# Ten full-array fp32 products of the identity, read by nothing, in TensorE's opening

## The chip, the cores and the metric

The kernel runs on one core of a Trainium2 chip. A core has five engines that run side by side and wait for one another by semaphores: TensorE (PE in the profile; its weight loads are shown apart as PEld), VectorE (DVE), ScalarE (ACT), GpSimd (POOL) and SyncE (SP), which here only issues transfers. The metric is the time of one execution on the device in microseconds (us), as the median of several runs.

## The reference, cut to what matters

One layer of a hybrid encoder is applied to two inputs with shared weights: a prompt of 512 tokens and a sample of 1024 tokens, 1024 channels each, all in fp32.

```python
def encoder_layer(x, norm_g, w_in, qn_a, kn_a, rpb_a, qn_b, kn_b, sink_b, w_o_a, w_o_b, w_out, t5_table):
    h = rmsnorm(x, norm_g)
    proj = h @ w_in
    qa, ka, va, za, qb, kb, vb, zb, ga, gb = jnp.split(proj, np.cumsum(SPLITS)[:-1], axis=-1)
    ...
    oa = neighbourhood_attention(qa, ka, va, rpb_a) * jax.nn.silu(za)
    oa = oa @ w_o_a
    ...
    ob = window_gqa_attention(qb, kb, vb, t5_table, sink_b) * jax.nn.silu(zb)
    ob = ob @ w_o_b
    merged = jax.nn.sigmoid(ga) * oa + jax.nn.sigmoid(gb) * ob
    return x + merged @ w_out
```

Before anything else can be multiplied, h must exist: each token's 1024 channels are scaled by one over the root of their mean square and by the gain norm_g.

## The kernel before, in words

Every large product is made of three TensorE products: each fp32 operand is split into a high part and a rest (whi and wlo for weights, hh and hl for h), and the kernel adds whi·hh, wlo·hh and whi·hl. ScalarE makes the high parts by a copy into the reduced type, VectorE or GpSimd subtracts to get the rests.

The prompt comes first (norm, projections, two attentions, dense part), then the sample. In the opening, which is all that the change touches, the work is this:

- Two constants are made: the identity `ident` (128 by 128, GpSimd, by a helper in masks.py) and a row of ones (VectorE, L417). The row of norm gains is fetched to one partition (L1621) and spread over 128 partitions by four fp32 products with the row of ones (L1629, contraction over one row, 256 columns each; the trace holds two records for each fp32 product).
- The prompt is normed in four tiles t of 128 tokens (`norm_tile`). For each: ScalarE squares and sums the tile (L460), GpSimd makes the scale (L464, L468), VectorE multiplies by scale and gain (L520), TensorE transposes blocks of 128 by 128 with `ident` (L532), ScalarE copies the result to hh (L537), VectorE makes hl (L542). Tile t=0 goes in four pairs of blocks, k0 = 0, 2, 4, 6; the other tiles in two halves of four blocks.
- The projection of tile t (L761, stationary operand from h, 384 columns of weights moving) takes eight blocks k with three products each. Its weights come in pieces of two blocks; ScalarE makes whi (L602), VectorE or GpSimd wlo (L607).
- ScalarE also copies the spread gain from PSUM to SBUF for the later tiles (L1641).

What sets the order: the class `Flow` collects all operations with a priority, an assumed cost and their dependencies, plays the program through once with these costs while it is being built, and issues each operation on its engine in the order in which it started there. The order on each engine is thus fixed when the kernel is built; on the chip each engine takes its own list strictly in turn, and semaphores hold an instruction until its inputs are there. A `bank("d")` is the one PSUM bank of the kind d; banks x and p are of other kinds.

In the kernel before, a function `wake` stands ready to issue pairs of transposes into a d bank, but its count WAKE is 0, so it issues nothing.

Of the kernel before, what the change touches and what calls it, by code (L numbers as in the profile page):

```python
# [29 lines left out]
SIDE = {5: 0, 8: 1, 11: 2, 15: 3}  # L30
CLASSIC_S = (1, 0, 2)
LEFT_PAD = 56
WAKE = 0
SOON = 10
RAW = {512: 2, 1024: 1}
WAKE_PRIO = 2
START = (-10, -6.5, -4, -3)
GATE = 2
FIRST_POOL = (0,)
# [1 line left out]
P = 128  # L41
# [313 lines left out]
def encoder_kernel(  # L355
# [26 lines left out]
    pe = nc.tensor  # L382
# [7 lines left out]
    ident = cpool.tile([P, P], F32, tag="ident", name="ident")  # L390
# [38 lines left out]
    f = Flow(pspool)  # L429

    def bank(tag):
        return f.value(pspool, [P, 512], F32, tag, BANKS[tag])
# [3 lines left out]
    gx_v = Value(None, None, None, "gx", 1)  # L436
    line_op, expanded = [], {}

    def wake():

        ps = bank("d")
        for i in range(WAKE):
            f.op(
                (("pe", 427),),
                lambda e, i=i: [pe.transpose(ps.t[:, j * P : (j + 1) * P], ident, ident) for j in range(2)],
                WAKE_PRIO, **({"into": [ps]} if i else {"new": [ps]}),
            )

    def rstd(pool, x, t, prio, load_prio, bufs, after=(), load_after=(), out=None):

        val = lambda shape, dt, tag, n: f.value(pool, shape, dt, tag, n)
        xt = val([P, D], F32, "xt", bufs)
        junk = val([P, D], mybir.dt.bfloat16, "junk", 1)
        ss, v = (val([P, 1], F32, "n" + n, bufs) for n in "sv")
        r = out or val([P, 1], F32, "nr", bufs)
        rv = lambda: r.t[:, t : t + 1] if out else r.t
        f.dma(lambda: nc.sync.dma_start(xt.t, x[t * P : (t + 1) * P, :]), 524288, load_prio, new=[xt], after=load_after)
        f.op(
            (("act", ACT_(D) + 93),),
            lambda e: act.activation(junk.t, xt.t, AF.Square, accum_out=ss.t), prio, new=[junk, ss], use=[xt], after=after,  # L460
        )
        f.op(
            (("pool", 164),),
            lambda e: nc.gpsimd.tensor_scalar(v.t, ss.t, 1.0 / D, EPS, op0=ALU.mult, op1=ALU.add),  # L464
            prio, new=[v], use=[ss],
        )
        f.op(
            (("pool", 464),), lambda e: nc.gpsimd.tensor_tensor(rv(), v.t, mhalf[:, :1], op=ALU.pow),  # L468
            prio, use=[v], **({"into": [r]} if out and t else {"new": [r]}),
        )  # L470
        return xt, r
# [33 lines left out]
    def norm_tile(pool, x, gb, gains_row, hh, hl, t, prio, load_prio, after=(), load_after=()):  # L505

        xt, r = rstd(pool, x, t, prio, load_prio, 4, after, load_after)
        tok = slice(t * P, (t + 1) * P)
        step, out = 2 if t == 0 else 4, []
        for k0 in range(0, KC, step):  # L510
            n, cols, ks = step * P, slice(k0 * P, (k0 + step) * P), slice(k0, k0 + step)
            ps, made = gains_row[k0 // 4]
            if t == 0:
                c = slice(k0 % 4 * P, k0 % 4 * P + n)
                gv, kw = lambda ps=ps, c=c: ps.t[:, c], {"use": [r], "hold": [xt, ps], "after": [made[k0 % 4 // 2]]}
            else:
                gv, kw = lambda cols=cols: gb.t[:, cols], {"use": [r], "hold": [xt, gb], "after": made, "port": True}
            m = f.op(
                (("dve", DVE_(n) + 60),),
                lambda e, cols=cols, gv=gv: dve.scalar_tensor_tensor(  # L520
                    xt.t[:, cols], xt.t[:, cols], r.t, gv(), op0=ALU.mult, op1=ALU.mult
                ),
                prio, **kw,
            )
            if t == 0:
                made.append(m)
            ps = bank("x")

            def emit(e, k0=k0, ps=ps):
                for i in range(step):  # L530
                    k = k0 + i
                    pe.transpose(ps.t[:, i * P : (i + 1) * P], xt.t[:, k * P : (k + 1) * P], ident)  # L532

            f.op((("pe", 109 * step),), emit, prio, new=[ps], after=[m], hold=[xt])
            pv = lambda ps=ps, n=n: ps.t[:, :n].rearrange("p (k n) -> p k n", n=P)
            a = f.op(
                (("act", ACT_(n, False)),), lambda e, ks=ks, pv=pv: act.activation(hh.t[:, ks, tok], pv(), AF.Copy),  # L537
                prio, use=[ps], hold=[hh],
            )
            b = f.op(  # L540
                (("dve", DVE_(n)),),
                lambda e, ks=ks, pv=pv: dve.tensor_tensor(  # L542
                    hl.t[:, ks, tok], pv(), hh.t[:, ks, tok].bitcast(F32), op=ALU.subtract
                ),
                prio, use=[ps], after=[a], hold=[hh, hl],
            )
            out += [a, b]
        return out
# [1067 lines left out]

    f.stage(-1000, open=(r_h, d0["p"], rb_pool, early["p"], late["p"], norm_p), make=h_p)
    f.dma(lambda: nc.sync.dma_start(gx, norm_g), 4096, 1, into=[gx_v])
    wake()
    gb = f.value(rb_pool, [P, NT_S], F32, "rb", 1)  # L1620
    row = f.dma(lambda: nc.sync.dma_start(gb.t[:1], norm_row.unsqueeze(0)), 4096, START[0] + 0.1, new=[gb])  # L1621
    gains_row = []
    for i in range(2):
        ps, made = bank("x"), []
        for j in range(2):
# [3 lines left out]
                lambda e, ps=ps, cols=cols, out=out: pe.matmul(ps.t[:, out], one, gb.t[:1, cols], start=True, stop=True),  # L1629
# [3 lines left out]
    for t in range(gp.nb):  # L1633
        h_ops["p"][t] = norm_tile(
            norm_p, x_p, gb, gains_row, *h_p, t, NORM[t], START[t], h_ops["p"][t - GATE][::2] if t >= GATE else (),
            h_ops["p"][0][-1:] if t > 1 else (),
        )
        for i, (ps, users) in enumerate(gains_row if t == 0 else ()):
            gains_row[i][1] = [f.op(
                (("act", ACT_(512, False)),),  # L1640
                lambda e, ps=ps, i=i: act.activation(gb.t[:, i * 512 : i * 512 + 512], ps.t, AF.Copy),  # L1641
                NORM[1] - 1, use=[ps], hold=[gb], after=users[2:],
            )]
    setup(norm_p, -0.7, h_ops["p"][1][:1])
    expand_ops(gp, [max(-1, (h // 2 - 1) * gp.nb) for h in range(8)], [h_ops["p"][t][:1] for t in (1, 3, 3, 3)])
    o_p, exps, start = attention_phase(gp, *h_p, h_ops["p"], mask_p, early["p"], late["p"])
    rb = f.value(rb_pool, [P, NT_S], F32, "rb", 1)
    r_s = f.value(norm_p, [P, gs.nb], F32, "r_s", 1)
    for t in range(gs.nb):
        at = 6 + 2 * t  # L1650
        rstd(norm_p, x_s, t, at, at, 4, (), [f.begun[NT_P, at - 2]], r_s)
    ps, r_t = bank("x"), f.value(norm_p, [gs.nb, P], F32, "r_t", 1)
# [4 lines left out]
    o = f.dma(lambda: nc.sync.dma_start(r_d, r_t.t), 4096, 20, use=[r_t])  # L1657
    f.dma(
        lambda: nc.sync.dma_start(rb.t, r_d.rearrange("t p -> (t p)").partition_broadcast(P)), 524288, 24, new=[rb],
        after=[o, f.begun[NT_P, 23]],  # L1660
# [21 lines left out]
    o_s, exps, start = attention_phase(gs, *h_s, h_ops["s"], mask_s, early["s"], late["s"])  # L1682
# [89 lines left out]
```

## Time and profile before

| | |
|---|---|
| median of 3 runs | 1145.79 us (1144.96 to 1147.68) |
| profiled execution, from the first to the last instruction (span) | 1144.7 us |
| what the runs' median has beyond this span | 1.1 us |
| TensorE busy in the span | 1133.8 us (99%) |
| VectorE, ScalarE, GpSimd busy | 854.4, 644.9, 308.3 us |
| TensorE busy in the first 30 us | 24.61 us |
| first product of the projection starts | 10.92 us |

Times in the trace are counted from the span's start. The profiled execution's own time is known by its span alone; it is compared with the runs through the 1.1 us in the table. In a timeline the first number is the start, the second how long the instruction or a merged group of them (xN) took. [...]

### The profile page before, as it was taken

What the parts mean: (1) busy time and instruction counts of PE and PEld (TensorE: products, weight loads), DVE (VectorE), ACT (ScalarE), POOL (GpSimd) and SP (SyncE); (2) the same over time, 40 slices, a digit from 0 to 9 for tenths busy, and PEclk for the clock granted to TensorE, in tenths of its full rate; (3) what the DMA queues carried; (4) which work ended last, traced back from release to release, by engine and by line L of the source; (5) the groups of instructions that cost most, each with busy time, mean ns of one, the idle gap of its engine ahead of it and who ended that gap; (6) DMA issues with size and microseconds to landing.
All of it is one profiled execution on the core that took longest, in us unless ns stands there. A gap on an engine that the chain in (4) does not pass through costs nothing.

```text
span 1144.7 us, 18482 instructions
## 1 busy us (share of the span) xinstructions
PE 1133.8 (99%) x6139; PEld 985.8 (86%) x6139; DVE 854.4 (75%) x1975; ACT 644.9 (56%) x1467; POOL 308.3 (27%) x413
## 2 busy tenths in 40 slices
PE   8999999999999999999999999999999999999998
PEld 6999988888888899999999888888888888788887
DVE  5888798497765468887778888865878755497984
ACT  5777987544433346665678988865534434343320
POOL 3653433000010054343333445330222210132110
PEclk9999999999999999999999999999999999999999
DMA  7854543488786422121221213226657335573072
GB/s 253 273 158 141 181 113 102 115 264 266 232 277 199 165 72 67 25 70 32 71 61 50 56 37 93 56 66 214 218 148 211 129 111 159 200 238 121 29 223 90
DMA packets 124705, 159.86 MB, mean 140 GB/s; under 512 B 28297, under 2 KB 66961, under 8 KB 124610
## 3 DMA queue, kind: packets, MB, share of 16 engines
q1 hardware_dynamic: 124610, 158.69, 45.4%
q8 instruction: 48, 0.79, 0.3%
q14 instruction: 47, 0.39, 0.1%
HBM read 121.93 MB, written 41.44 MB: 143 GB/s over the span
## 4 chain that ended last, share of the span: by engine, by line
PE 94%; DVE 2%; DMA 2%; ACT 1%; POOL 1%; issue 0%; SPq 0%; ACTq 0%; POOLq 0%
PE p L761 25%; PE x L1285 9%; PE x L1286 9%; PE x L1284 9%; PE x L1063 5%; PE x L1026 5%; PE x L934 4%; PE p L1284 4%; PE p L1285 4%; PE d L1284 4%; PE p L1286 4%; PE d L1286 4%; PE d L1285 4%; PE x L861 2%; DMA ot<-u_d 1%; DMA w<-in_w_att_dram 1%
## 5 line engine op out<-in xcount | busy, mean ns | idle before, releaser
L761 PE MATMUL p<-whi,hh 128*128 128x384 f32 x384 | 133.4, 348 | 0.0
L761 PE MATMUL p<-wlo,hh 128*128 128x384 f32 x384 | 133.1, 347 | 0.0
L761 PE MATMUL p<-whi,hl 128*128 128x384 f32 x384 | 132.4, 345 | 0.0
L978 ACT ACTIVATE sb<-sb,mx 128x384 f32<-128x384 f32 (+1 forms) x192 | 107.5, 563 | 22.4 <-DVE mx L969 22.2
L1167 ACT ACTIVATE whi<-raw 128x512 fp32r<-128x512 f32 (+1 forms) x140 | 81.1, 590 | 52.6 <-PE x L1285 26.2
L761 PE MATMUL p<-whi,hb 128*128 128x384 f32 x384 | 107.5, 347 | 0.0
L1172 POOL TENSOR_TENSOR wlo<-raw,whi 128x512 fp32r<-128x512 f32 (+1 forms) x29 | 40.9, 1413 | 242.4 <-ACT whi L1167 130.4
L1284 PE MATMUL x<-hh,whi 128*128 128x512 f32 x264 | 102.7, 389 | 0.0
L1285 PE MATMUL x<-hl,whi 128*128 128x512 f32 x264 | 102.7, 389 | 0.0
L1286 PE MATMUL x<-hh,wlo 128*128 128x512 f32 x264 | 102.7, 389 | 0.0
L1037 DVE TENSOR_TENSOR pp<-x,pp 128x512 fp32r<-128x512 f32 (+1 forms) x136 | 82.6, 638 | 18.9 <-ACT pp L1032 17.8
L1172 DVE TENSOR_TENSOR wlo<-raw,whi 128x512 fp32r<-128x512 f32 (+1 forms) x111 | 70.1, 645 | 30.5 <-ACT whi L1167 30.2
L1285 PE MATMUL x<-T,whi 128*128 128x512 f32 x224 | 87.5, 390 | 0.3 <-DVE T L1172 0.2
L1286 PE MATMUL x<-T,wlo 128*128 128x512 f32 x224 | 87.2, 389 | 0.0
L1284 PE MATMUL x<-T,whi 128*128 128x512 f32 x224 | 87.1, 389 | 0.0
L1032 ACT ACTIVATE pp<-x 128x512 fp32r<-128x512 f32 (+1 forms) x136 | 70.9, 560 | 22.8 <-PE x L1026 21.8
L799 POOL TENSOR_TENSOR rs_r<-rs_v,mhalf 128x4 f32<-128x4 f32 (+1 forms) x72 | 81.7, 1134 | 5.7
L1063 PE MATMUL x<-pp,v 128*128 128x256 f32 (+1 forms) x368 | 77.8, 324 | 0.8 <-DVE pp L1037 0.8
L792 POOL TENSOR_SCALAR rs_v<-ss 128x4 f32<-128x4 f32 (+1 forms) x72 | 26.2, 364 | 187.3 <-DVE ss L785 184.6
L761 PEld LDWEIGHTS p<-whi,hl 128*128 128x128 f32 x384 | 73.0, 190 | 1.3 <-issue 1.0
L761 PEld LDWEIGHTS p<-wlo,hh 128*128 128x128 f32 x384 | 73.0, 190 | 1.0 <-issue 0.5
L761 PEld LDWEIGHTS p<-whi,hh 128*128 128x128 f32 x384 | 73.0, 190 | 0.9 <-issue 0.5
(351 smaller groups left out, 2985.5 us busy)
## 6 DMA issues: line engine op xcount, KB each, us to landing
raw<-in_w_g_dram SPq DMA_DIRECT2D x76, 256.0 KB
w<-in_w_att_dram SPq DMA_DIRECT2D x46, 384.0 KB
ot<-o_d SPq DMA_DIRECT2D x36, 256.0 KB
g_d<-C SPq DMA_DIRECT2D x34, 256.0 KB
raw<-in_w_z_dram SPq DMA_DIRECT2D x32, 256.0 KB
raw<-in_w_out_dram SPq DMA_DIRECT2D x32, 256.0 KB
C<-g_d SPq DMA_DIRECT2D x24, 256.0 KB
out_dram<-C SPq DMA_DIRECT2D x23, 256.0 KB
```

What stands on the lines that cost most here:

```text
L761: pe.matmul(ps.t[:, :GW], part[u](k), mv.t[:, c], start=k == 0 and m == 0, stop=k == KC - 1 and m == 2,)
L799: lambda e: nc.gpsimd.tensor_tensor(r.t[:, :nn], rv.t[:, :nn], mhalf[:, :nn], op=ALU.pow),
L978: act.activation(sb.t[:, :width], sb.t[:, :width], AF.Exp, bias=mx.t[:, i : i + 1], scale=-1.0, accum_out=sm.t[:, i : i + 1],)
L1026: pe.transpose(pt.t[:, u * P : (u + 1) * P], sbs[i].t[:, c * P : (c + 1) * P], ident)
L1032: lambda e, pt=pt, pp=pp, nn=nn: act.activation(pp.t[:, 0, :nn], pt.t[:, :nn], AF.Copy),
L1037: lambda e, pt=pt, pp=pp, nn=nn: dve.tensor_tensor(pp.t[:, 1, :nn], pt.t[:, :nn], pp.t[:, 0, :nn].bitcast(F32), op=ALU.subtract),
L1063: pe.matmul(out(), v.t[:, vs], mv(), start=first, stop=last)
L1167: (("act", ACT_(n)),), lambda e: act.activation(hi(), src(), AF.Copy), prio,
L1172: lambda e: engines[e].tensor_tensor(lo(), src(), hi().bitcast(F32), op=ALU.subtract), prio,
L1284: pe.matmul(out, hi.t[:, cs], mh(), start=first and k == 0, stop=False)
L1285: pe.matmul(out, hi.t[:, cs], ml(), start=False, stop=False)
L1286: pe.matmul(out, lo.t[:, cs], mh(), start=False, stop=last and k == len(ws) - 1)
```

## The change

`wake` now issues plain fp32 products instead of transposes: the identity as the stationary and as the moving operand, 128 rows by 128 columns, into one d bank that no one reads. It is called twice. Seven products are put at the front of the whole program by their priority; three follow the second pair of transposes of tile t=0. The scheduler is told that they cost nothing, so that everything else is placed as before.

```diff
-WAKE = 0
+WAKE = (7, 3)
...
-WAKE_PRIO = 2
...
-    def wake():
-
-        ps = bank("d")
-        for i in range(WAKE):
+    idle = bank("d")
+
+    def wake(n, prio, after=()):
+
+        for _ in range(n):
             f.op(
-                (("pe", 427),),
-                lambda e, i=i: [pe.transpose(ps.t[:, j * P : (j + 1) * P], ident, ident) for j in range(2)],
-                WAKE_PRIO, **({"into": [ps]} if i else {"new": [ps]}),
+                (("pe", 0),), lambda e: pe.matmul(idle.t[:, :P], ident, ident, start=True, stop=True), prio, after=after,
+                **({"into": [idle]} if idle.writers else {"new": [idle]}),
             )
...
-            f.op((("pe", 109 * step),), emit, prio, new=[ps], after=[m], hold=[xt])
+            o = f.op((("pe", 109 * step),), emit, prio, new=[ps], after=[m], hold=[xt])
+            if t == 0 and k0 == 2:
+                wake(WAKE[1], -1000, [o])
...
-    wake()
+    wake(WAKE[0], -1000)
```

The order on TensorE at the start of the program, before: x is a PSUM bank, rb and one the gain row and the row of ones, xt the normed tile, p the projection's bank.

```order
L1762 UNCONDITIONAL_BRANCH [waits barrier_Pool_Activation_PE_DVE_SP_release]
L1629 MATMUL x<-rb,one 128x256 [waits DMAHW1_49,DVE_49]
L1629 MATMUL x<-rb,one 128x256 x3
L532 MATMUL x<-ident,xt 128x128 [waits DMAHW0_49,DVE_49]
L532 MATMUL x<-ident,xt 128x128
L532 MATMUL x<-ident,xt 128x128 [waits DVE_49]
```

The same place in the changed kernel, in which L444 is the line of the new products, L1630 answers to L1629 and L531 to L532:

```order
L1763 UNCONDITIONAL_BRANCH [waits barrier_Pool_Activation_PE_DVE_SP_release]
L444 MATMUL d<-ident 128x128 [waits Pool_49]
L444 MATMUL d<-ident 128x128 x6
L1630 MATMUL x<-rb,one 128x256 [waits DMAHW1_49,DVE_49]
L1630 MATMUL x<-rb,one 128x256 x3
L531 MATMUL x<-ident,xt 128x128 [waits DMAHW0_49,DVE_49]
L531 MATMUL x<-ident,xt 128x128
L531 MATMUL x<-ident,xt 128x128 [waits DVE_49]
L531 MATMUL x<-ident,xt 128x128
L444 MATMUL d<-ident 128x128 x3
L531 MATMUL x<-ident,xt 128x128 [waits DVE_49]
```

Seven products stand ahead of the four that spread the gain, and wait only for GpSimd to have made the identity; three stand between the second and the third pair of transposes, with no wait of their own. These three rows are all that is new: on TensorE and on the other four engines every other instruction has the place and the waits that it had (up to line numbers, which move by one).

## The prediction

> **What bounds the kernel now.** I read the page first, to see which engine is full and which carries the chain that ended last; then TensorE by stretches, and what it waited for.
>
> ```profile
> PE 1133.8 (99%) x6139; PEld 985.8 (86%) x6139; DVE 854.4 (75%) x1975; ACT 644.9 (56%) x1467; POOL 308.3 (27%) x413
> PE 94%; DVE 2%; DMA 2%; ACT 1%; POOL 1%; issue 0%; SPq 0%; ACTq 0%; POOLq 0%
> 0.00:30.00 30.00, 24.61 (x115) 21.21 (x116) 17.31 (x43) 17.79 (x34) 12.47 (x23) 1.00 0.74 252
> 30.00:60.00 30.00, 29.50 (x192) 27.37 (x191) 25.10 (x81) 22.96 (x56) 19.77 (x31) 1.00 0.83 274
> 60.00:100.00 40.00, 40.00 (x263) 37.37 (x262) 32.20 (x96) 28.44 (x76) 21.49 (x35) 1.00 0.53 159
> ```
>
> TensorE bounds the kernel: 94% of the chain is its own work, and from 30 us on it hardly stops (29.50 of 30.00, then 40.00 of 40.00 us). So what shortens its opening without a new wait should come off the end too. The first 30 us hold 5.4 us of idleness. The timeline of TensorE shows more than idleness there: its pace changes (start, length; the distance of starts is the pace).
>
> ```profile
> 4.42 3.75 PE L1629 MATMUL x<-rb,one 1*128 1x256 f32 x8 [4.42 <-DMA rb<-in_norm_row_dram]
> 8.10 1.11 PE L532 MATMUL x<-ident,xt 128*128 128x128 f32 x4
> 10.13 1.14 PE L532 MATMUL x<-ident,xt 128*128 128x128 f32 x4 [0.92 <-DVE xt L520]
> 10.92 0.67 PE L761 MATMUL p<-whi,hh 128*128 128x384 f32 x1
> ...
> 15.23 0.52 PE L761 MATMUL p<-wlo,hh 128*128 128x384 f32 x1
> 15.55 0.52 PE L761 MATMUL p<-whi,hl 128*128 128x384 f32 x1
> 15.87 0.74 PE L532 MATMUL x<-ident,xt 128*128 128x128 f32 x4
> 16.36 0.43 PE L761 MATMUL p<-whi,hh 128*128 128x384 f32 x1
> 16.63 0.34 PE L761 MATMUL p<-wlo,hh 128*128 128x384 f32 x1
> 16.80 0.34 PE L761 MATMUL p<-whi,hl 128*128 128x384 f32 x1
> ...
> 17.50 0.33 PE L761 MATMUL p<-whi,hh 128*128 128x384 f32 x1
> 17.67 0.60 PE L532 MATMUL x<-ident,xt 128*128 128x128 f32 x4
> 18.03 0.42 PE L761 MATMUL p<-wlo,hh 128*128 128x384 f32 x1
> 18.29 0.33 PE L761 MATMUL p<-whi,hl 128*128 128x384 f32 x1
> ```
>
> Products of one shape start 0.32 us apart up to 15.87 and 0.17 apart from 16.63 on; four transposes take 0.49 at 15.87 (to the start of the next product) and 0.36 at 17.67. So TensorE runs at about half pace until some 16.0 us. The column PEclk above says 1.00 for the first 30 us all the same: this start-up state is read from the distances only. Between 10.92 and 16.0 TensorE pays about 5.1 · (1 − 0.17/0.32) = 2.4 us for it, and only there: earlier it waits for others. That 2.4 us is the prize, if the ten products raise the pace sooner.
>
> [...]
>
> **The change part by part.** What the opening hangs on beside TensorE stands in the timelines of the other engines:
>
> ```profile
> 0.99 0.29 POOL masks.py:199 TENSOR_SCALAR_AFFINE_SELECT ident<-ident 128x128 f32<-128x128 f32 x1
> 6.68 0.87 DVE L520 SCALAR_TENSOR_TENSOR xt<-xt,nr,x 128x256 f32<-128x256 f32 x2 [5.68 <-PE x L1629]
> 7.84 0.85 ACT L602 ACTIVATE whi<-w 128x768 fp32r<-128x768 f32 x1 [1.72 <-DMA w<-in_w_att_dram]
> 8.59 0.58 ACT L1641 ACTIVATE rb<-x 128x512 f32<-128x512 f32 x1
> 8.72 0.96 DVE L607 TENSOR_TENSOR wlo<-w,whi 128x768 fp32r<-128x768 f32 x1 [1.17 <-ACT whi L602]
> 9.60 0.86 DVE L520 SCALAR_TENSOR_TENSOR xt<-xt,nr,x 128x256 f32<-128x256 f32 x2
> 10.35 0.91 ACT L537 ACTIVATE hh<-x 128x256 fp32r<-128x256 f32 x3
> 10.75 1.09 DVE L542 TENSOR_TENSOR hl<-x,hh 128x256 fp32r<-128x256 f32 x3 [0.29 <-ACT hh L537]
> 11.76 0.74 DVE L520 SCALAR_TENSOR_TENSOR xt<-xt,nr,rb 128x512 f32<-128x512 f32 x1
> 12.41 0.95 DVE L607 TENSOR_TENSOR wlo<-bias,whi 128x768 fp32r<-128x768 f32 x1
> 13.28 0.42 DVE L542 TENSOR_TENSOR hl<-x,hh 128x256 fp32r<-128x256 f32 x1
> 13.62 0.95 DVE L607 TENSOR_TENSOR wlo<-bias,whi 128x768 fp32r<-128x768 f32 x1
> 14.48 0.75 DVE L520 SCALAR_TENSOR_TENSOR xt<-xt,nr,rb 128x512 f32<-128x512 f32 x1
> 17.28 0.69 DVE L542 TENSOR_TENSOR hl<-x,hh 128x512 fp32r<-128x512 f32 x1 [2.05 <-ACT hh L537]
> ```
>
> ```profile
> L1629 PE MATMUL x<-rb,one x8: 629/629/761, 4.4 to 7.5; 1*128 1x256 f32 x8
> 11.07 0.33 PEld L761 LDWEIGHTS p<-wlo,hh 128*128 128x128 f32 x1
> ```
>
> The first of these two rows groups the records that spread the gain (shortest, middle and longest in ns, first and last start), the second is one weight load at the low pace.
>
> *Seven products first.* The identity is ready at 0.99 + 0.29 = 1.28; a wait across engines costs about 0.1 (VectorE's first multiply of the pair at 9.60 ends near 10.03, TensorE goes on at 10.13), so they start at about 1.4. The trace of before has no such product. The nearest row is the four fp32 products at 4.42, eight records of 256 columns, the first at 4.42 and the last at 7.5: (7.5 − 4.42)/7 = 0.44 apart, so 0.22 for 128 columns. Fourteen records make 3.1 us, to 4.5. The gain row lands at 4.42, so the spreading products start at most 0.1 late. Both ends: at full pace half of it, 1.5 us, done long before 4.42; and, were a slow weight load of 0.33 (the row above) never hidden, 14 · (0.33 + 0.22) = 7.7 us, to 9.1. I take 3.1, because the eight records at 4.42 hide their loads. What covers a delay: VectorE is done with the spread gain at 6.68 + 0.87 = 7.55, and the next that needs TensorE's result from there, ScalarE at 8.59, is held by its own copy and that by a weight transfer (7.84). So about 0.9 us of delay costs nothing; each further us costs one.
>
> *Three products in the gap.* Six records, 1.3 us at half pace, from about 8.95 (four transposes from 8.10, each taken like a record of 128 columns, 0.21 to 0.22) to 10.3; the next transposes start at 10.13. At worst 0.15 late, and the third piece of hh, which needs them, is not before 10.95 in ScalarE's row of three at 10.35. At full pace they end at 9.6. Cost nothing; without that cover, 0.15.
>
> *What a full pace would be worth.* hh cannot start before 10.35 (ScalarE: weight transfer, copy, gain copy, sum of the second tile), so the first projection product stays at 10.92. From there TensorE would run at 0.17, until VectorE holds it. VectorE works without a pause from 10.75 to 15.23, and nothing in that row waits for a late TensorE result. Step by step: 13 products bring TensorE to 10.92 + 13 · 0.173 = 13.17; the next needs the wlo that ends at 12.41 + 0.95 = 13.36, so it starts at 13.46. Two products, to 13.81; four transposes, 14.17; four products (the first behind transposes takes 0.26), 14.95; three more, whose wlo is there at 14.57, to 15.46. Then come the transposes of the second half of tile t=1, whose input is ready at 15.23: they start at 15.46 in place of 17.67. That is 2.2 us. The cap is 17.67 − 15.33 = 2.34, since VectorE's row doesn't move; the floor is 0, if the pace does not change. I take 2.2, the step-by-step value.
>
> *Whether it is kept.* Behind 17.67 the chain is handed on by TensorE itself: hl of t=1 waited 2.05 us for ScalarE, and ScalarE for the transposes. Up to 31 us one row could catch it:
>
> ```profile
> 22.28 1.42 DVE L520 SCALAR_TENSOR_TENSOR xt<-xt,nr,rb 128x512 f32<-128x512 f32 x2 [0.48 <-POOL nr L468]
> 30.87 0.41 PE L861 MATMUL x<-ident,qk 128*128 128x128 f32 x2 [0.50 <-DVE qk L816]
> 37.65 0.29 DVE L695 TENSOR_TENSOR bias<-mask,raw 128x128 f32<-128x128 f32 x1 [1.05 <-DMA raw<-rpb_x]
> ```
>
> From 22.28 VectorE is full and TensorE waits for it once, before 30.87 (the 0.50 us missing in 30 to 60). But 22.28 itself hangs on sums that ScalarE makes behind the first projection's results, so the whole stretch moves along. The transfer at 37.65 is issued behind VectorE's work and moves too, and TensorE doesn't wait for it. I count 2.2 kept.
>
> Sum: 0 + 0 − 2.2 on a span of 1144.7 gives 1142.5; the runs' median lies 1.1 above that span, so **1143.6 us**.
>
> **The rivals.**
>
> *The pace does not rise before the projection.* TensorE was busy in the trace of before from 4.42 to 9.21 without a rise; the rise came 5.1 us after the first product over 128 rows that isn't a transpose. So the one-row products and the transposes may not count as work. Then the ten leave holes: 3.1 us of counted work, nothing from 4.5 to 8.95, 1.3 us, a hole of 0.7. At best the three start the count at 8.95 in place of 10.92, the rise comes 2.0 us sooner, and that is worth 2.0 · 0.47 = 0.9; at worst nothing. Time 1144.9 to 1145.8, middle 1145.3. Against it: 4.8 us may simply have been too short.
>
> [...]
>
> *The gain is caught later.* VectorE's full stretch from 22.28 or the transfers behind it do not move, TensorE waits 2 us longer at 30.87: 1145.2 to 1145.8. For it: VectorE is as full as TensorE there. Against: what releases that stretch.
>
> *Slower: the seven products hold back the gain.* If each record pays its weight load in full, they end at 9.1 and the spreading starts 4.7 late; 0.9 is covered, 3.8 is not, and the first projection product moves from 10.92 to about 14.7: 1149.6 if the pace stays low. It decides from 5.3 us on as the end of the seven. For it: slow loads of 0.33 are longer than the 0.22 of a record. Against: at 4.42 loads were hidden.
>
> **How the numbers follow.** Forecast 0.56, low pace 0.28, caught later 0.09, slower 0.07. A measurement of this kernel can tell about 0.2%, 2.29 us, so faster means under 1143.50. The forecast lies on that edge, and its cap of 2.34 just beyond it; but the before's moment of rise was seen once and the runs of before spread over 2.7 us, so I give it 0.27 faster and 0.29 same. Low pace gives 0.04 and 0.24, caught later 0.02 and 0.07, slower 0.07 all but a rest that I neglect: faster 0.33, same 0.60, slower 0.07. Range: forecast alone 1142.6 to 1144.6; with low pace and late catch, 1142.4 to 1146.0.
>
> **What would show it.** Right: fourteen records on bank d from 1.4 to 4.5; 128-row products 0.17 apart from 10.92; two short waits of TensorE for wlo by 15; the transposes of 17.67 at 15.5, the row of 30.87 at 28.7. The low-pace rival: 0.32 apart beyond 13 us. The slower one: the spreading later than 5.3. Caught later: 17.67 moved, 30.87 not. The forecast is wrong if the first projection product moves off 10.9 by more than 0.3, or the clock falls back in the hole before it.

## The result, and the profile after

| | before | after |
|---|---|---|
| median | 1145.79 us (17 runs, 1144.67 to 1150.25) | 1149.2 us (17 runs, 1146.57 to 1151.39) |
| profiled execution, span | 1144.7 us | 1146.6 us |
| ratio of the runs | | 1.0022, 95% interval 1.0013 to 1.0031 |

The change costs 3.4 us between the medians; the ratio is taken over all the runs and so is a little smaller than that of the medians, 1.0030. The prediction, 1143.6 us with a range up to 1146.0, was wrong. The profiled execution of after took 1148.39 us by its own time, 1.8 us more than its span.

The opening first. The timeline of TensorE in the changed kernel (start, length, line, operation; xN is a merged group; in brackets the idle time before it and what ended it):

```profile
1.34 3.35 PE L444 MATMUL d<-ident 128*128 128x128 f32 x14 [1.34 <-POOL ident masks.py:199]
4.68 3.75 PE L1630 MATMUL x<-rb,one 1*128 1x256 f32 x8
...
9.27 1.49 PE L444 MATMUL d<-ident 128*128 128x128 f32 x6
...
11.26 0.67 PE L762 MATMUL p<-whi,hh 128*128 128x384 f32 x1
...
12.04 0.52 PE L762 MATMUL p<-whi,hl 128*128 128x384 f32 x1
12.36 0.41 PE L762 MATMUL p<-whi,hh 128*128 128x384 f32 x1
12.61 0.34 PE L762 MATMUL p<-wlo,hh 128*128 128x384 f32 x1
...
29.40 0.41 PE L862 MATMUL x<-ident,qk 128*128 128x128 f32 x2 [0.50 <-DVE qk L817]
```

The ten products stand where they were put. The first projection product starts at 11.26 (10.92 before) still at half pace (the products of 12.04 and 12.36 are 0.32 apart); the pace rises at about 12.4 (0.17 apart from 12.61 on), against 16.0. (The trace also notes the granted clock, but only from its first change on, which is a change to 1.00 at 12.50 us here and at 16.15 in before; so the 1.00 that the table by stretches gives for the time ahead of it is no reading.) So the row of 30.87 starts at 29.40: at 30 us the changed kernel leads by 1.5 us. It ends 1.9 us behind. In the view of TensorE's waits by what ended them (us in total, times, longest) one row has grown; of before, then of after:

```profile
PE x L861 <- DVE qk L816: 1.0, 2, 0.5
```

```profile
PE x L862 <- DVE qk L817: 3.1, 4, 1.8
```

It is the wait of the transposes of q and k for VectorE, from 1.0 to 3.1 us. I followed the same products through both traces; the lead of 1.5 us shrinks to 1.0 at 58 us and to 0.7 near 100, turns into a lag of 0.6 at 404 us, 1.0 at 422 and 1.8 at 518, and stays there to the end. The largest step is at 404. The chain of waits there (start, length; what the next step waited for), of before:

```profile
395.11 4.21 DMA fr<-in_w_g_dram
399.32 0.02 issue
399.34 0.64 ACT fh L1167
...
403.68 0.44 DVE qk L816
404.12 0.04 issue
404.16 0.44 PE x L861 x2
```

and of after:

```profile
394.42 5.85 DMA fr<-in_w_g_dram
400.27 0.02 issue
400.30 0.64 ACT fh L1168
...
404.26 0.44 DVE qk L817
404.70 0.04 issue
404.74 0.44 PE x L862 x2
```

Everything between the load and TensorE takes no longer than before (4.47 us against 4.84). The load of w_g took 1.64 us longer (5.85 against 4.21), and so what was 0.7 ahead at its issue is 1.0 behind when it lands. The trace records a load in sixteen parts: in after fifteen have landed by 398.24 and the last comes at 400.27; in before all lie between 398.26 and 399.32. The two transfers issued next (395.36 and 396.29) have one late part as well in after, each 2.0 us behind the other fifteen. The load is of the same size, on the same queue, over 380 us behind the change.

What is different in that stretch is in the view of the transfers. The rows are queue and kind, packets, MB, and share of the sixteen engines' time; first before, from the issue of the load just ahead of this one (394.63) to ScalarE's start (399.34), then after (393.94 to 400.30):

```profile
q1 hardware_dynamic: 624, 1.33, 82.9%
```

```profile
q1 hardware_dynamic: 743, 1.62, 78.1%
q8 instruction: 1, 0.02, 0.9%
```

A fetch of instructions stands inside the load in after (its record in the trace starts at 397.90 and takes 0.96 us); in before it comes at 400.18, behind the landing. The row doesn't say whose code it is; the counts of the page give a reckoning. Its rows of after (engines' instructions; the queue's fetches and MB):

```profile
PE 1136.9 (99%) x6159; PEld 988.8 (86%) x6159; DVE 853.9 (74%) x1975; ACT 644.7 (56%) x1467; POOL 308.3 (27%) x413
...
q8 instruction: 48, 0.79, 0.3%
```

48 fetches bring 0.79 MB, 16 KB each. TensorE has 2 · 6159 records, 257 for each fetch (before: 2 · 6139, 256), and no other engine has so many. From these counts I take the fetches for TensorE's code, in pieces of about 256 instructions while the kernel runs: an estimate, which the experiment with 256 instructions more agrees with (49 fetches). The ten products are 20 records more on PE and 20 on PEld: 40 instructions, so by this estimate every later fetch begins 40 instructions earlier in what was the program before, and is due earlier against the loads (397.90 for 400.18 here). Whether that is the cause is what the experiments were for.

The step at 518 us shows the same. A load of a bias is issued (SPq) and VectorE adds it; before, then after:

```profile
513.43 0.33 SPq L682 DMA_DIRECT2D raw<-rpb_x  x1
...
516.35 1.03 DVE L695 TENSOR_TENSOR bias<-mask,raw 128x192 f32<-128x192 f32 x4
```

```profile
514.43 0.33 SPq L683 DMA_DIRECT2D raw<-rpb_x  x1
...
517.86 1.58 DVE L696 TENSOR_TENSOR bias<-mask,raw 128x192 f32<-128x192 f32 x4 [0.55 <-DMA raw<-rpb_x]
```

VectorE starts 2.9 us after the issue in before and never waits; in after it is 3.4 us and it waits 0.55. TensorE's code is fetched at 515.32 in after, inside the load, and at 519.34 in before, behind it. Here too one part of the load is late in after: fifteen have landed by 516.76, the last comes at 517.77; in before all have landed by 515.76.

### The profile page after: what moved, and what is told of

Same layout as the page of the kernel before. It is cut to its first block, busy times and chain, and to the rows that moved or that the text cites. A ratio compares the mean times of both kernels' runs of the same rounds, so it can differ in the third digit from the quotient of the medians.

```text
span 1146.6 us, 18522 instructions
## 1 busy us (share of the span) xinstructions
PE 1136.9 (99%) x6159; PEld 988.8 (86%) x6159; DVE 853.9 (74%) x1975; ACT 644.7 (56%) x1467; POOL 308.3 (27%) x413
## 4 chain that ended last, share of the span: by engine, by line
PE 91%; DMA 2%; DVE 2%; ACT 2%; POOL 1%; issue 1%; SPq 0%; POOLq 0%; ACTq 0%; DVEq 0%
PE p L762 23%; PE x L1286 9%; PE x L1287 9%; PE x L1285 9%; PE x L1064 5%; PE x L935 4%; PE x L1027 4%; PE p L1285 4%; PE p L1286 4%; PE p L1287 4%; PE d L1285 4%; PE d L1286 4%; PE d L1287 4%; PE x L862 2%; DMA ot<-u_d 1%; DMA xt<-in_x_s_dram 1%
```

## The experiments

Three theories stood at the start. *Opening*: a faster opening brings loads into each other's way later on, whatever made it faster. *Banks*: the new bank d, made first, moves the PSUM banks of all others. *Code*: the added instructions cost, whatever they do; from the second round on this is made definite: they move TensorE's code fetches into loads. A fourth, *Count* (any added instruction costs), was added in the second round. All kernels but one ran in five rounds beside the kernel before.

**The change once more.** No edit.

> The changed kernel once more, beside the kernel before on one chip. Three theories of the loss. Opening: the ten products bring the opening forward by 1.5 us, and the transfers that later work waits for then land later by more than that (the load of fr at 395 us took 4.21 us to land before, 5.85 us after the change). Banks: the product's d bank is now made first, so that every PSUM bank of the kernel has moved by one place, and that costs. Code: twenty more records of TensorE ahead of the rest, whatever they do. All three: ratio 1.002 to 1.003 again. If the loss was one of the chip or of the day: below 1.001. A second profile shows whether the gain of 1.5 us at 30 us is lost at the same places (58, 97, 404, 422 and 518 us) or at others.

Measured: 1149.4 us, ratio 1.0024 (1.0012 to 1.0036). The result stands. The load of w_g again took 5.83 us, with a fetch in it at 397.52, and here the wait had a sequel. TensorE's timeline:

```profile
405.34 0.44 PE L862 MATMUL x<-ident,qk 128*128 128x128 f32 x2 [2.06 <-DVE qk L817]
...
406.08 0.52 PE L762 MATMUL p<-whi,hl 128*128 128x384 f32 x1
406.40 0.52 PE L762 MATMUL p<-whi,hh 128*128 128x384 f32 x1
...
409.26 0.33 PE L762 MATMUL p<-whi,hh 128*128 128x384 f32 x1
409.43 0.33 PE L762 MATMUL p<-wlo,hh 128*128 128x384 f32 x1
```

After the wait of 2.06 us the products are 0.32 us apart until 409.26: the pace has fallen back to half for some 3.4 us, and the lag grows from 1.2 to 2.7 us. This time the granted clock says so: the row of 406 to 408 us in the table by stretches (length; busy time and instructions of PE, PEld, DVE, ACT, POOL; PEclk; DMA) shows 0.50.

```profile
406.00:408.00 2.00, 2.00 (x7) 2.00 (x7) 1.53 (x6) 0.60 (x3) 1.98 (x3) 0.50 0.00 0
```

The granted clock changes at 405.81 and 409.22 us in this trace, 3.41 apart. The changed kernel with the old banks, which follows, shows the same after a wait of 2.05 us: a granted clock of 0.50 from 406.08 us for 3.41 us.

**Banks alone, and the products with the old banks.** The first edit is put in the kernel before, the second in the changed one:

```diff
+    pspool.tile([P, 512], F32, tag="d", name="d", bufs=BANKS["d"])
```

```diff
+    for tag in "xp":
+        for _ in range(BANKS[tag]):
+            pspool.tile([P, 512], F32, tag=tag, name=tag, bufs=BANKS[tag])
```

> The kernel before with none of the ten products; the d bank alone is made first, so that all PSUM banks have the places of the changed kernel (d in bank 0, x in 1 to 5, p in 6 and 7, in place of x in 0 to 4, p in 5 and 6, d in 7). Every instruction, order and wait is that of the kernel before. Opening: ratio 1.000. Code: 1.000. Banks: 1.003 or more, since the opening's gain is missing too.

> The changed kernel with its ten products in full, but with the banks x and p made first, so that all PSUM banks have the places of the kernel before (x in 0 to 4, p in 5 and 6, d in 7). Opening or Code: ratio 1.002 to 1.003. Banks: the opening's gain comes out, 0.998 to 0.9995.

Measured: banks alone 1146.31 us, ratio 1.0004 (0.9987 to 1.002); the products with the banks of before 1149.56 us, ratio 1.0022 (1.0011 to 1.0034). Moving the banks costs nothing that can be measured, and undoing it helps nothing. *Banks* falls.

**The ten products cut to one row and one column.** They stand in the same places with the same instructions, and take next to no time (fourteen records 0.49 us and six 0.29, for 3.35 and 1.49 in after).

```diff
-                (("pe", 0),), lambda e: pe.matmul(idle.t[:, :P], ident, ident, start=True, stop=True), prio, after=after,
+                (("pe", 0),), lambda e: pe.matmul(idle.t[:1, :1], ident[:, :1], ident[:, :1], start=True, stop=True), prio, after=after,
```

> The changed kernel with its ten products cut to one row of output and one column (the identity's first column with itself), at the same places: same number of instructions, but next to no work for TensorE. PSUM places as in the changed kernel. Opening: pace rises at about 16 us as before, ratio 1.000. Banks or Code: 1.002 to 1.004 although the opening is as before.

Measured: 1148.43 us, ratio 1.0016 (1.0005 to 1.0027). Most of the loss is there although TensorE is barely occupied by the ten, which speaks for *Code*. One trace did not show all of it as expected: near 404 us nothing was lost. The fetch began at 397.46, 0.7 us before the w_g load had landed, and the late part (399.89, 1.1 us behind the other fifteen) is one of the next transfer, a store of C issued at 395.10, which TensorE does not wait for. At 518 us 1.0 us was lost, for 0.8 in after, with a fetch (513.20) in the load of the bias. The rest of the 1.5 us by which this trace ends behind the first trace of before was lost behind 600 us, and I didn't follow it. VectorE's and TensorE's waits near 518 us:

```profile
516.11 1.57 DVE L696 TENSOR_TENSOR bias<-mask,raw 128x192 f32<-128x192 f32 x4 [0.80 <-DMA raw<-rpb_x]
518.16 0.41 PE L862 MATMUL x<-ident,qk 128*128 128x128 f32 x2 [0.86 <-DVE qk L817]
```

**A second trace of the kernel before.** No edit.

> The kernel before, unchanged: a second trace of it, to see what differs between two executions of one program. Both theories expect the same: TensorE starts its work near 404 us and 518 us without a wait of 1 us or more, code fetches near 400 and 519 us as in the first trace (to about 1 us), a span of 1144 to 1146 us. If it shows waits near 404 or 518 us too, neither theory explains anything and the losses are chance.

Measured: 1146.53 us, span 1144.7. No wait of 1 us near 404 or 518, fetches at 400.84 and 519.54. Along the way TensorE lags the first trace by 0.6 to 0.8 us (from 97 to 970 us) and ends level: so steps of 0.6 us in one trace are chance.

**The same columns in three wide products, and with small ones behind them.** 896 columns in the opening and 384 in the gap, as products of 512, 384 and 384 columns (the identity repeated as the moving operand): 12 instructions more than before instead of 40. The second kernel adds seven products of one row and one column, which makes it 40 again.

```diff
-WAKE = (7, 3)
+WAKE = ((512, 384), (384,))
...
-        for _ in range(n):
+        for n in cols:
+            rhs = ident[:, :n] if n <= P else ident.unsqueeze(1).broadcast_to([P, n // P, P])
...
```

```diff
-WAKE = ((512, 384), (384,))
+WAKE = ((512, 384, 1, 1, 1, 1, 1), (384, 1, 1))
```

> The same columns of identity products (896 ahead of the gain row, 384 in the gap) in three wide products instead of ten narrow ones: 12 more instructions on TensorE instead of 40. Code (the code fetches come earlier and meet loads): the fetches move by about a third of what they did, the one near 400 us stays behind the landing of the w_g load, nothing is lost near 404 us and little near 518 us, the 1.5 us won by 30 us are mostly kept: ratio 0.9985 to 0.9997. Opening (an earlier opening itself makes later loads land late): as with ten products, losses near 404 and 518 us, ratio 1.0015 to 1.003.

> As the three wide products, and seven products of one column and one row behind them (five in the opening, two in the gap), so that TensorE has 40 more instructions again, with the opening of the wide version. Code: the losses near 404 and 518 us are back, ratio 1.0015 to 1.003, against 0.9985 to 0.9997 for the wide version alone. Opening: the same as the wide version alone.

Measured: wide 1145.99 us, ratio 0.9996 (0.998 to 1.0011); wide with small ones 1148.24 us, ratio 1.0014 (1.0002 to 1.0026). Seven products that do nothing, 28 instructions, cost about 2.2 us between the medians. The wide kernel's TensorE and ScalarE rows:

```profile
1.34 3.31 PE L447 MATMUL d<-ident 128*128 128x512 f32 x4 [1.34 <-POOL ident masks.py:199]
4.58 1.99 PE L1633 MATMUL x<-rb,one 1*128 1x256 f32 x8
...
10.29 0.67 PE L765 MATMUL p<-whi,hh 128*128 128x384 f32 x1
...
11.54 0.33 PE L765 MATMUL p<-wlo,hh 128*128 128x384 f32 x1
...
396.44 0.64 ACT L1171 ACTIVATE fh<-fr 128x512 fp32r<-128x512 f32 x1 [0.32 <-DMA fr<-in_w_g_dram]
```

ScalarE waits 0.32 us for the w_g load, no fetch stands between its issue and its landing (the fetch comes at 397.68), and the lead of 2.5 us at 30 us is 2.6 at 518. With the small ones added, the same row, TensorE's wait and the transfers from 395.11 (the issue of the load just ahead) to ScalarE's start:

```profile
400.46 0.63 ACT L1171 ACTIVATE fh<-fr 128x512 fp32r<-128x512 f32 x1 [1.39 <-DMA fr<-in_w_g_dram]
...
405.26 0.44 PE L865 MATMUL x<-ident,qk 128*128 128x128 f32 x2 [1.15 <-DVE qk L820]
```

```profile
q1 hardware_dynamic: 698, 1.53, 81.7%
q8 instruction: 1, 0.02, 1.4%
```

The fetch (397.72) is in the load again and TensorE waits 1.15 us. Of the 2.4 us that this trace lost, 0.6 lies at 404 and 0.8 at 518 us; 1.0 was lost by 58 us, behind a load of x that met a code fetch only in its last 0.3 us, so there the cause is open. The openings of these two traces differ too (28.33 and 30.34 for the row of 30.87; after a first 3.41 us at full clock the granted clock was 0.50 for 3.41 us in the wide trace and for 6.83 in the other), so *Opening* is told apart best by the next kernel and by the small products above, which lose with no faster opening than the unchanged kernel may have.

**A whole fetch of small products.** 64 of them, 50 in the opening and 14 in the gap, are 256 instructions, so by the estimate above each later fetch holds what it held before.

```diff
-WAKE = (7, 3)
+WAKE = (50, 14)
```

(on the kernel with the ten small products)

> Sixty-four products of one row and one column (50 in the opening, 14 in the gap) and no full ones: 256 more instructions on TensorE, which is one whole fetch of its code, so that every later fetch holds the same instructions as in the kernel before. The 14 cost about 0.5 us in the gap, the 50 about 0.4 us ahead of the gain row. Code (the places of the fetches): no loss near 404 and 518 us, fetches near 400.2 and 519.3 us again, ratio 0.9997 to 1.0008. Count (any more instructions cost): six times the 1.6 thousandths of the ten small products, 1.005 or more. Opening: as the ten small products, 1.0016.

Measured: 1146.75 us, ratio 1.0001 (0.999 to 1.0012). Six times the added instructions of the ten small products, and no loss can be told. Taken by itself the pair is not far apart (the intervals, 1.0005 to 1.0027 and 0.999 to 1.0012, overlap), but a loss in proportion to the instructions, which needs 1.005 or more, is out. *Count* falls, and with it *Opening* as the source of these losses. The page and the timeline:

```profile
q8 instruction: 49, 0.80, 0.3%
```

```profile
399.05 0.63 ACT L1168 ACTIVATE fh<-fr 128x512 fp32r<-128x512 f32 x1 [0.30 <-DMA fr<-in_w_g_dram]
...
403.84 0.44 PE L862 MATMUL x<-ident,qk 128*128 128x128 f32 x2 [0.55 <-DVE qk L817]
```

One fetch more, the others at 399.81 and 518.60 as in before (400.18, 519.34), and no new wait in either place. This trace lost 1.7 us behind 970 us for another reason, which I didn't follow; its own time, 1147.81 us, is above its median.

**Half a fetch, and the wide version again.** 32 small products, 128 instructions:

```diff
-WAKE = (50, 14)
+WAKE = (25, 7)
```

> Thirty-two products of one row and one column (25 in the opening, 7 in the gap) and no full ones: 128 more instructions on TensorE, half of one fetch of its code, so that the fetches that stood near 400.2 and 519.3 us come about half the distance of two fetches, some 12 us, earlier. Code: the w_g load of 394 to 399 us and the loads around 515 us meet no fetch, so TensorE waits at most 0.6 us near 404 and 518 us, as before; another load may be met in another place, so the ratio lies anywhere from 0.9997 to 1.0016. Count (each instruction more costs): the losses grow in proportion to those of the ten small products (40 instructions, 1.0016), to 1.005, waits near 404 and 518 us among them.

> The three wide products once more, to tell whether this version beats the kernel before, and whether its pace rises as early in a second trace. Code: ratio 0.9985 to 1.0000, no wait of 1 us near 404 or 518 us; the gain row's products are 0.22 us apart again, and TensorE leads the kernel before by 1 to 2.5 us at 31 us. Opening: 1.0015 to 1.003.

Measured: half a fetch 1148.04 us, ratio 1.001 (1.0001 to 1.0019); wide 1146.55 us, ratio 1.0008 (0.9994 to 1.0021). With 128 instructions the waits at 404 and 518 us are gone (0.24 us and none), and new ones stand where before has none. In the new places a load of w_att and one of line_d, in before:

```profile
95.59 0.86 ACT L602 ACTIVATE whi<-w 128x768 fp32r<-128x768 f32 x1
...
117.20 0.61 ACT L662 ACTIVATE bias<-raw 128x384 f32<-128x384 f32 x1 [0.32 <-DMA raw<-line_d]
```

and with the 32 small products, where the transfers of 114.13 to 119.13 follow:

```profile
96.75 0.84 ACT L603 ACTIVATE whi<-w 128x768 fp32r<-128x768 f32 x1 [0.96 <-DMA w<-in_w_att_dram]
...
119.13 0.62 ACT L663 ACTIVATE bias<-raw 128x384 f32<-128x384 f32 x1 [1.73 <-DMA raw<-line_d]
```

```profile
q1 hardware_dynamic: 765, 0.96, 72.0%
q8 instruction: 1, 0.02, 1.2%
q14 instruction: 1, 0.01, 0.7%
```

TensorE's code was fetched at 93.88 and 116.97 here, inside both loads; neither trace of before has a fetch of it between 88 and 100 or 110 and 122 us. A third place, near 41 us, cost 0.8 us: a fetch at 38.34 lies in a load of w_att, whose last part came at 40.66, 0.9 us behind the others. The loss follows the fetch. The wide version's second trace falls short of what I expected (a ratio of 1.0000 at most, a lead of 1 us or more at 31 us; it leads by 0.6). It has no wait near 518 us, but a step of 1.1 us near 408, behind a late mask load (0.6 in the first wide trace). No fetch of TensorE's code stands inside that load (400.65 to 405.81); two of 8 KB on the other instruction queue, q14, do (402.12, 1.5 us, and 402.20, 0.3 us), and whether they count I didn't follow. Over both rounds it can't be told from the kernel before, so no version here beats it.

All traces side by side. The first three times are starts of the same TensorE rows in each; "lost" is how much the row of 518 us fell back against the row of 30 us, compared with before (518.14 − 30.87 = 487.27); the wait is ScalarE's for the late w_g load; the last column is the start of TensorE's code fetch against that load's last part.

| kernel | added instructions | ratio | row of 30 us | 404 us | 518 us | lost | ScalarE's wait | fetch |
|---|---|---|---|---|---|---|---|---|
| before, first trace | 0 | 1 | 30.87 | 404.16 | 518.14 | 0 | 0.81 | 0.9 behind |
| before, second trace | 0 | 1 | 30.69 | 404.79 | 518.76 | 0.8 | 0.64 | 0.9 behind |
| banks alone | 0 | 1.0004 | 29.88 | 402.69 | 516.75 | −0.4 | 0.36 | 1.1 behind |
| after | 40 | 1.0022 | 29.40 | 404.74 | 519.92 | 3.3 | 2.37 | 2.4 ahead |
| after, again | 40 | 1.0024 | 29.76 | 405.34 | 521.88 | 4.9 | 2.49 | 3.1 ahead |
| old banks | 40 | 1.0022 | 29.88 | 405.52 | 522.38 | 5.2 | 2.51 | 3.7 ahead |
| ten small | 40 | 1.0016 | 30.03 | 402.71 | 518.16 | 0.9 | 0.65 | 0.7 ahead |
| wide and small | 40 | 1.0014 | 30.34 | 405.26 | 520.04 | 2.4 | 1.39 | 2.7 ahead |
| wide | 12 | 0.9996 | 28.33 | 401.00 | 515.56 | 0 | 0.32 | 1.3 behind |
| wide, again | 12 | 1.0008 | 30.26 | 403.32 | 518.42 | 0.9 | 0.22 | 0.9 behind |
| 64 small | 256 | 1.0001 | 30.01 | 403.84 | 517.76 | 0.5 | 0.30 | 0.8 behind |
| 32 small | 128 | 1.0010 | 30.10 | 405.75 | 519.67 | 2.3 | 0.34 | 12.3 ahead, another load |

In the four traces in which the fetch began 2.4 to 3.7 us before the load's end, ScalarE waited 1.4 to 2.5 us; in the other eight 0.2 to 0.8. The five results with 40 added instructions and the one with 128 have their interval above 1; the four with 0, 12 and 256 have 1 inside it. And it is not this load alone: in the twelve traces together, 3300 loads of inputs can be followed part by part, and the last part landed over 1 us behind the fifteenth in 70 of the 405 in which a fetch of TensorE's code began between the issue and the fifteenth part, against 41 of the 2895 others. What is shown is that the losses go with the place of the fetches; why one part of a load comes late there, no run shows. The ten full products lose somewhat more than the small ones (1.0022 to 1.0024 against 1.0014 and 1.0016), but the intervals overlap, so whether their work adds to it stays open; in two of the three traces with full products 1.5 us of the loss is the spell at half pace.

## Why the prediction was wrong

*Seven products first*: about right. Fourteen records took 3.35 us for the 3.1 that I counted, 0.24 apart; the gain row's products started 0.26 late for at most 0.1.

*Three products in the gap*: undercounted. The first four transposes ended later by that 0.26, the three started at 9.27 for 8.95, and the first projection product moved to 11.26. That is 0.34 late for 0 ("Cost nothing; without that cover, 0.15"), past the 0.3 that I had named as a sign that the forecast is wrong.

*What a full pace would be worth*: the sign was right, the size not. That the projection starts at 10.92 and runs at 0.17 from there did not happen: the pace rose at 12.4, and in the two other traces with ten full products near 13.3. The 2.2 us of the sum rest on a full pace from the projection's first product, which no run shows: in all twelve traces the second and third product of the projection are still 0.32 us apart. By the granted clock the pace rose at 12.50, 13.27 and 13.55 us in these three, and between 14.04 and 16.15 in the six traces without full products. The row of 30.87 came 1.5, 1.1 and 1.0 us earlier in these three, for 2.2. And before's one trace was a poor base: the traces that had no full product in the opening (before again, banks alone, 10, 32 and 64 small ones) have it 0.2, 1.0, 0.8, 0.8 and 0.9 us earlier than the trace that I worked from. Against the mean of these five and that trace itself, 0.6, the ten products gain about 0.6 us (1.2 − 0.6). I had written that the moment of rise "was seen once", and still took it as the base.

*Whether it is kept* is the step that failed: "I count 2.2 kept", from rows up to 38 us, with each added instruction taken to cost its time on TensorE and nothing else. With the 40 instructions the code fetches stood elsewhere (397.90 for 400.18, 515.32 for 519.34), and loads some 400 and 500 us later came late: in the traces with ten full products 3.3 to 5.2 us were lost between 30 and 518 us (0.5 to 0.8 of it by 58 us, where I didn't follow the cause). What is kept was bounded at zero on the losing side; it should have been open: in the trace of after the lag of 1.8 us at 518 us was still there at the end.

*The sum*: the base was low as well. In all runs whose span is on record, those of before among them (its second trace: 1146.53 by its own time, span 1144.7), 1.7 to 1.9 us lie beyond the span, for the 1.1 that I took from the median. With 1.8 the same sum gives 1144.3, still 4.9 below what was measured.

*The rivals*. Low pace had the opening half right: the pace did not rise before the projection, and it rose 2.7 to 3.6 us sooner than in before's trace, for the 2.0 that I allowed at best (0.5 to 3.7 sooner by the granted clock, against the six traces without full products). Its time, 1144.9 to 1145.8, was wrong by the same omission. The gain caught later was right in kind, and I gave it 0.09; but I looked for it behind 22.28 or 37.65, where nothing was caught (30.87 moved to 29.40), and let it take back the gain only. The products holding back the gain row did not happen (4.68, and it would have had to be past 5.3). Slower by over 0.2% had 0.07 from that rival alone.

Whether one-row products and transposes count as work for the rise, no run here tests by itself. The moment isn't fixed by the program: the changed kernel rose at 12.50 us in one trace and at 13.27 in another. In the wide kernel the pace is full at 4.58 (records 0.22 apart), half again at 10.29 and full from about 11.3.

## What to carry to other kernels

Here instructions that do nothing weren't free even where the engine that runs them waits: ten products of one row and one column, 40 instructions, cost 1.6 thousandths (1.0016), and the code fetch near 400 us stood at 397.46 with them for 400.18. So look for the instruction queue's rows inside the loads that end waits. Before believing in a gain or a loss of a few tenths of a per cent, run the same number of added instructions without the work, and a number that makes a whole fetch (here 256 instructions, 1.0001). Take a start-up moment that differs between traces of one program, as the rise of the pace does here (12.50 and 13.27 us), from several of them, not from one.

## What the hardware showed that I had not expected

Code is fetched during the run in 48 pieces of 16 KB (before and after), by my estimate TensorE's, one for about 256 of its instructions, and each took 0.9 to 2.0 us in these two traces. The w_g load that holds the start of such a fetch 2.4 to 3.7 us before its end took 4.85 to 5.85 us from issue to last part, in four traces, for 3.7 to 4.3 in the other eight. It is late by its last part alone, 0.8 to 2.0 us behind the fifteenth, for at most 0.3 in the others.

The pace of TensorE fell back to half for about 3.4 us after a single wait of 2.06 us, in the middle of a stretch that is otherwise full, and the spell cost 1.5 us on top of the wait; the same happened after a wait of 2.05 us in the trace with the old banks. After a wait of 1.79 us (the profiled run of after) it did not.

In the traces, the rows behind wide and narrow products of the same columns did not have the same pace. After four records of wide ones, 3.31 us, the eight gain-row records took 1.99 us (1.99 in its second trace, 2.19 with the small ones behind); after fourteen records of 128 columns, 3.35 us, they took 3.75 to 3.78 in all three traces. The weight loads were busy 2.66 us of the first 4 with narrow products and 1.17 with wide ones. By the granted clock the first change, to 1.00, came at 4.46, 4.54 and 5.38 us with wide products, and at 12.50, 13.27 and 13.55 with narrow ones. But this does not show that the width decides: there are three traces of each, and no run changed the width alone. Over all runs the mean granted clock was below 1.000 in 16 of 35 with wide products and in 20 of 40 with ten narrow ones (a later spell at half pace counts too), against 12 of 131 without full products: by this neither kind stands out.
